# Low parts of every second expert block made by an accumulating DMA instead of GpSimd or VectorE

## The chip, the cores and the metric

The kernel runs on one core of a Trainium2 chip. The metric is the device time of one execution in microseconds (us). Its engines are TensorE (PE in the rows; PEld is its weight load), VectorE (DVE), ScalarE (ACT), GpSimd (POOL) and SyncE (SP, which here only issues DMAs).

## The reference, cut to what matters

A two-layer network on 512 positions of width 1024, all in float32. Each layer is a mixer followed by a PEER sub-layer, a retrieval among 128 x 128 = 16384 one-neuron experts:

```python
def block(xb):                                   # 128 positions
    q = (xb @ wq).reshape(128, 8, 2, 128)
    s1 = einsum('phd,kd->phk', q[:, :, 0], k1)   # scores of 128 keys, twice
    s2 = einsum('phd,kd->phk', q[:, :, 1], k2)
    ...                                          # top 16 of each, top 16 of their sums
    ue, ve = u_tab[eid], v_tab[eid]              # 8 heads x 16 experts per position
    act = gelu(einsum('pd,phkd->phk', xb, ue))
    return einsum('phk,phkd->pd', softmax(top_s) * act, ve)
```

## The kernel before, in words

For three of the four tiles of 128 positions (384 columns) the kernel does not gather: it multiplies by all experts and weighs by a mostly empty matrix. A block is one first key, 128 experts. `u_item(b)` multiplies the block's 128 x 1024 rows of `peer_u` by the activations and leaves the GELU in `act`; `v_item(b)` multiplies the weighted GELUs by `peer_v` and sums in `acc`. The fourth tile's rows are gathered with indirect DMAs (`gather`, buffers `grow_`), issued by GpSimd and consumed by VectorE.

To keep float32 precision, every weight is split into a high part (the value rounded to `F32R`) and a low part (what is left), and a product is three matmuls (`mm3`, L125 to L128): high by high, high by low, low by high. `weights` loads a block into `raw` (SyncE's queue), ScalarE writes `hi` by a copy (L112), and VectorE or GpSimd writes `lo = raw - hi` (L115). The third matmul of a block's first k (L128, `u<-hh,lo`) is the first to read `lo`. `raw` has two buffers, `hi` and `lo` three each. The argument `sub` says who subtracts:

```python
raw = st.tile([P, D], F32, name="raw", bufs=2)
nc.sync.dma_start(out=raw, in_=src)
hi = st.tile([P, D], F32R, name="hi", bufs=3)
lo = st.tile([P, D], F32R, name="lo", bufs=3)
split(hi, lo, raw, A, sub)
```

The PEER part of a layer runs in this order:

- The query loop: 16 blocks of `wq`; blocks 1 and 10 (`j % QM == 1`) get their low part from GpSimd.
- The first expert loop: `u_item` for blocks 0 to 31 (`FIRST` = 32). GpSimd subtracts for the odd blocks, VectorE for the even ones. After block 8i VectorE ranks the last scores (`best`), after block 8i + 1 it runs `pick` for one tile of positions: the top 16 of the sums, the softmax and the indices, with one exponential on ScalarE (L576) and three transposes on TensorE (L620 to L622). `ahead(items, n)` writes the loads of block b + n ahead of block b's matmuls. In this loop the order on each engine is set by the framework's planner, which goes by priority (the order of the code) and by the times that it reckons.
- The hand-ordered steps (`manual_schedule`): `PLAN` lists blocks 32 to 63 of u with 2 gathers, 64 blocks of v with 100, blocks 64 to 127 of u with 58, and 64 blocks of v with the rest. `run` prepares the weights of step i + 2 (`LOOK`) in the middle of step i (`meanwhile`), together with `spread` (small matmuls that make the weight matrix, L683 and L684), `weigh` (L698, L700) and `onehots` (L668 to L675). VectorE subtracts in all these steps.

In both, buffers are handed out when the program is planned: a new tile takes the buffer that the plan frees first, and its first writer waits for the last reader of that buffer.

Of the kernel before, what the change touches and what calls it, by code (L numbers as in the profile page):

```python
# [10 lines left out]
F32 = mybir.dt.float32  # L11
# [5 lines left out]
AF = mybir.ActivationFunctionType  # L17
OP = mybir.AluOpType
# [19 lines left out]
CH = NK // 2  # L38
# [14 lines left out]
UM = 2  # L53
# [3 lines left out]
FIRST = 2 * UNIT  # L57
# [9 lines left out]
def trunk(ctx: ExitStack, tc: tile.TileContext, x, rows1, rows2, ada, w_qk, w_row, w_o, wq, kt, wst,  # L67
          vnorm, fnorm, ut, u_rows, v_rows, out):
    nc = tc.nc
    V, A, G, T = nc.vector, nc.scalar, nc.gpsimd, nc.tensor  # L70
# [39 lines left out]
    def split(dst_hi, dst_lo, src, eng=A, sub=V):  # L110
        if eng is A:
            A.activation(dst_hi, src, AF.Copy)  # L112
        else:
            V.tensor_copy(dst_hi, src)  # L114
        sub.tensor_tensor(dst_lo, src, dst_hi.bitcast(F32), OP.subtract)  # L115

    def weights(src, sub=V):
        raw = st.tile([P, D], F32, name="raw", bufs=2)
        nc.sync.dma_start(out=raw, in_=src)
        hi = st.tile([P, D], F32R, name="hi", bufs=3)  # L120
        lo = st.tile([P, D], F32R, name="lo", bufs=3)
        split(hi, lo, raw, A, sub)
        return hi, lo

    def mm3(o, lh, ll, rh, rl, first, last):  # L125
        T.matmul(o, lh, rh, start=first, stop=False)  # L126
        T.matmul(o, lh, rl, start=False, stop=False)  # L127
        T.matmul(o, ll, rh, start=False, stop=last)  # L128

    def ahead(items, n=1):  # L130
        ready = []
        for i in range(len(items) + n):
            if i < len(items):
                ready.append(items[i][0]())
            if i >= n:
                items[i - n][1](ready.pop(0))
# [82 lines left out]
    def mixer(l):  # L219
        with tc.tile_pool(name="mx", bufs=1) as mx:  # L220
# [29 lines left out]
            with tc.tile_pool(name="pps", bufs=8, space=PSUM) as ps, tc.tile_pool(name="nm", bufs=1) as nm:  # L250
# [23 lines left out]
                def qk_item(j):  # L274
                    def use(w):
                        wh, wl = w
                        pq = ps.tile([P, S], F32, name="b")
                        for k in range(KD):
                            sl = slice(k * P, (k + 1) * P)
                            mm3(pq, wh[:, sl], wl[:, sl], hh[:, k], hl[:, k], k == 0, k == KD - 1)  # L280
                        A.activation(qk[:, j], pq, AF.Copy, scale=0.125 if j < 4 else 1.0)
                        fill(2)
                    return lambda: weights(w_qk[l, j]), use

                def row_items(src, evict):
                    pr = {}

                    def item(kk):
                        def use(w):
                            wh, wl = [a.rearrange("p (a b) -> p a b", a=2) for a in w]  # L290
                            for t in range(NTT):
                                if kk == 0:
                                    pr[t] = ps.tile([P, 512], F32, name="b")
                                ts = slice(t * P, (t + 1) * P)
                                for i in range(2):
                                    k = 2 * kk + i
                                    mm3(pr[t], hh[:, k, ts], hl[:, k, ts], wh[:, i], wl[:, i],
                                        k == 0, k == KD - 1)
                                if kk == 3:
                                    evict(t, pr[t])  # L300
                            fill(2)
                        return lambda: weights(src[kk]), use
                    return [item(kk) for kk in range(4)]
# [103 lines left out]
            with tc.tile_pool(name="ops", bufs=8, space=PSUM) as ps, tc.tile_pool(name="rg", bufs=1) as rg:  # L407
                po = {}

                def out_item(half, kk):  # L410
                    def use(w):
                        wh, wl = [a.rearrange("p (a b) -> p a b", a=2) for a in w]
                        for t in ORDER:
                            if kk == 0:
                                po[t] = ps.tile([P, 512], F32, name="b")
                            ts = slice(t * P, (t + 1) * P)
                            for i in range(2):
                                k = 2 * kk + i
                                mm3(po[t], hh[:, k, ts], hl[:, k, ts], wh[:, i], wl[:, i], k == 0, k == KD - 1)
                            if kk == 3:  # L420
                                residual(row[0], po[t], t, half, mx.tile([P, 512], F32, name="tk", bufs=2))
                                if half == 1:
                                    stats(t, y[:, t])
                                    nc.sync.dma_start(out=xd[t], in_=held["xs"][:, t])
                        if half == 0 and kk == 0:
                            ynorm(ps, 1)
                            row[0] = gate_rows(rg.tile([P, D], F32, name="grow"), ps, "b", l, 0)
                        fill(3)
                    return lambda: weights(w_o[l, half, kk]), use

                row = [None]
                ahead([out_item(half, kk) for half in range(2) for kk in range(4)])
                fill(96)

    def peer(l):
        with tc.tile_pool(name="pe", bufs=1) as pe, \
# [19 lines left out]
            def spot(b):  # L456
                a, i = slot(b)
                return act[a][:, i]

            def u_item(b):  # L460
                def use(w, meanwhile=None):
                    uh, ul = w
                    turn[0] ^= 1
                    pu = ups.tile([P, 512], F32, name=f"u{turn[0]}")
                    for k in range(KD):
                        if k == MID and meanwhile is not None:
                            meanwhile()
                        sl = slice(k * P, (k + 1) * P)
                        mm3(pu[:, :ND], uh[:, sl], ul[:, sl], hh[:, k, :ND], hl[:, k, :ND], k == 0, k == KD - 1)
                    w, n = spot(b), gone[b]  # L470
                    if n:
                        g = pe.tile([P, ND], F32, name="gu", bufs=1)
                        A.activation(g[:, :n], pu[:, :n], AF.Gelu_apprx_tanh)  # L473
                        late.append(lambda: V.tensor_mul(w[:, :n], w[:, :n], g[:, :n]))
                    if n < ND:
                        A.activation(w[:, n:], pu[:, n:ND], AF.Gelu_apprx_tanh)  # L476
                    known[b] = True
                return lambda: weights(ut[l, b], G if b < FIRST and b % UM == 1 else V), use

            with tc.tile_pool(name="tk", bufs=1) as tk, \  # L480
                    tc.tile_pool(name="tps", bufs=6, space=PSUM) as ps:
# [52 lines left out]
                def best(t, j0, s):  # L534
                    for jj in range(4):
                        j = j0 + jj
                        V.max(vals[t][:, j, 0:8], s[:, jj])
                        V.max_index(idx[t][:, j, 0:8], vals[t][:, j, 0:8], s[:, jj])
                        V.match_replace(s[:, jj], vals[t][:, j, 0:8], s[:, jj], NEG)
                        V.max(vals[t][:, j, 8:16], s[:, jj])  # L540
                        V.max_index(idx[t][:, j, 8:16], vals[t][:, j, 8:16], s[:, jj])
# [4 lines left out]
                with tc.tile_pool(name="pk", bufs=1) as pk:  # L546
# [82 lines left out]
                    def u_after(b):  # L629
                        prep, use = u_item(b)  # L630

                        def also(w):
                            use(w)
                            if b % 8 == 0:
                                best(*ranked.pop(0))
                            if b % 8 == 1:
                                pick(order[b // 8])
                        return prep, also

                    ahead([u_after(b) for b in range(FIRST)])  # L640

            with tc.tile_pool(name="gp", bufs=1) as gp, ExitStack() as psc:
                iot = gp.tile([P, P, SUB], F16, name="iot")
# [189 lines left out]
    for l in range(L):  # L833
        mixer(l)
        peer(l)
# [49 lines left out]
```

## Time and profile before

| | |
|---|---|
| median of 3 runs | 3236.4 us (3232.05 to 3236.57) |
| the profiled execution's own time | 3243.2 us |
| its span, first to last instruction | 3241.5 us |
| mean granted TensorE clock | 0.969 of full speed |
| busy: PE, DVE, ACT, POOL | 93%, 78%, 36%, 28% of the span |

All rows below are from the one profiled execution. A time of an engine's work is when the instruction ran; a DMA row's time to landing runs from its issue to the arrival of its last byte. Matmuls are pipelined, so the durations of successive ones overlap.

### The profile page before, as it was taken

The page shows a single profiled execution, that of the slowest core. Times are in us where ns is not written, and L with a number is a line of the kernel's source. Part 1 is how long each engine was busy: PE and PEld are TensorE (multiplying, and loading weights), DVE is VectorE, ACT ScalarE, POOL GpSimd, SP SyncE. Part 2 cuts the span into 40 slices and gives each one's busy share as a digit, 9 for nine tenths or more (in the row PEclk, how much of TensorE's full clock was granted, in tenths as well). Part 3 has the DMA queues.
Part 4 walks back from the last instruction along what each step waited for, and adds up shares of the span by engine and source line. Part 5 has one row for each costly group of instructions (what it writes and reads, how often), then busy time and mean ns, then how long its engine had stood idle before and what let it go on. Part 6 is the DMA issues. An engine that isn't in the chain of part 4 may idle for free. (4 is left out here: it accounts for less than half of the span.)

```text
span 3241.5 us, 46943 instructions
## 1 busy us (share of the span) xinstructions
PE 3022.1 (93%) x17516; PEld 2641.6 (81%) x17516; DVE 2536.8 (78%) x4973; ACT 1176.6 (36%) x2016; POOL 906.7 (28%) x602
## 2 busy tenths in 40 slices
PE   6998988999999999989989989889999999999897
PEld 5786887998777999867777878889977789997776
DVE  7677799698778889778744448979887788887787
ACT  3353333333333433323333533334333334333333
POOL 1001022103445223345410010220055432334452
PEclk8988999999999999999999899999999999999999
DMA  8746222337888666688732022233388876667885
GB/s 304 250 144 203 79 85 99 123 107 245 296 298 296 229 228 224 235 303 305 269 97 82 9 98 79 98 117 103 116 309 296 290 280 224 222 221 273 304 298 201
DMA packets 178840, 651.45 MB, mean 201 GB/s; under 512 B 19851, under 2 KB 20275, under 8 KB 178611
## 3 DMA queue, kind: packets, MB, share of 16 engines
q1 hardware_dynamic: 104018, 378.14, 34.2%
q0 software_dynamic: 73728, 268.47, 23.0%
q8 instruction: 137, 2.24, 0.3%
q10 hardware_dynamic: 864, 1.84, 0.2%
q14 instruction: 93, 0.75, 0.1%
HBM read 642.08 MB, written 6.29 MB: 200 GB/s over the span
## 5 line engine op out<-in xcount | busy, mean ns | idle before, releaser
L112 ACT ACTIVATE hi<-raw 128x1024 fp32r<-128x1024 f32 x600 | 635.9, 1060 | 1338.6 <-DMA raw<-in_v_rows 449.7
L115 DVE TENSOR_TENSOR lo<-raw,hi 128x1024 fp32r<-128x1024 f32 x564 | 699.0, 1240 | 230.8 <-ACT hi L112 229.6
L126 PE MATMUL u<-hh,hi 128*128 128x384 f32 x2048 | 706.4, 345 | 6.3 <-ACT act L476 6.3
L128 PE MATMUL u<-hh,lo 128*128 128x384 f32 x2048 | 692.8, 338 | 7.2 <-DVE lo L115 7.2
L127 PE MATMUL u<-hl,hi 128*128 128x384 f32 x2048 | 692.7, 338 | 0.0
L128 PE MATMUL acc<-hi,hl 128*128 128x512 f32 x1536 | 616.1, 401 | 63.1 <-DVE hl L115 61.4
L126 PE MATMUL acc<-hi,hh 128*128 128x512 f32 x1536 | 605.1, 394 | 9.7 <-ACT hh L112 9.7
L127 PE MATMUL acc<-lo,hh 128*128 128x512 f32 x1536 | 602.4, 392 | 0.0
L128 PEld LDWEIGHTS acc<-hi,hl 128*128 128x128 f32 x1536 | 290.4, 189 | 172.3 <-DVE hl L115 113.4
L128 PEld LDWEIGHTS u<-hh,lo 128*128 128x128 f32 x2048 | 389.9, 190 | 9.1 <-DVE lo L115 9.1
L126 PEld LDWEIGHTS u<-hh,hi 128*128 128x128 f32 x2048 | 390.3, 191 | 7.0 <-ACT act L476 6.9
L127 PEld LDWEIGHTS u<-hl,hi 128*128 128x128 f32 x2048 | 390.7, 191 | 0.1
L126 PEld LDWEIGHTS acc<-hi,hh 128*128 128x128 f32 x1536 | 290.8, 189 | 69.9 <-ACT hh L112 13.8
L127 PEld LDWEIGHTS acc<-lo,hh 128*128 128x128 f32 x1536 | 291.0, 189 | 62.0
L115 POOL TENSOR_TENSOR lo<-raw,hi 128x1024 fp32r<-128x1024 f32 x36 | 97.1, 2696 | 476.2 <-ACT hi L112 453.0
L126 PE MATMUL b<-hh,hi 128*128 128x512 f32 x384 | 150.7, 396 | 18.2 <-DVE hh L114 17.5
L127 PE MATMUL b<-hl,hi 128*128 128x512 f32 x384 | 150.3, 393 | 0.5 <-DVE hl L115 0.5
L128 PE MATMUL b<-hh,lo 128*128 128x512 f32 x384 | 150.1, 391 | 0.0
L190 DVE SCALAR_TENSOR_TENSOR aw<-aw,crow 128x1024 f32<-128x1024 f32 x96 | 119.1, 1244 | 37.8 <-DMA aw<-in_ada 37.5
L115 DVE TENSOR_TENSOR hl<-act,hh 128x384 fp32r<-128x384 f32 x256 | 140.9, 550 | 3.2 <-ACT hh L112 3.2
L473 ACT ACTIVATE gu<-u 128x384 f32<-128x384 f32 (+23 forms) x186 | 63.9, 343 | 208.9 <-PE u L128 208.3
L112 ACT ACTIVATE hh<-act 128x384 fp32r<-128x384 f32 x256 | 129.9, 508 | 4.8 <-PE acc L127 4.8
(1508 smaller groups left out, 4804.5 us busy)
## 6 DMA issues: line engine op xcount, KB each, us to landing
raw<-in_ut SPq DMA_DIRECT2D x256, 512.0 KB, 3.5
raw<-in_v_rows SPq DMA_DIRECT2D x256, 512.0 KB, 4.8
aw<-in_ada SPq DMA_DIRECT2D x96, 512.0 KB, 4.4
raw<-in_wq SPq DMA_DIRECT2D x32, 512.0 KB, 3.5
raw<-in_w_row SPq DMA_DIRECT2D x24, 512.0 KB, 4.4
raw<-in_w_qk SPq DMA_DIRECT2D x16, 512.0 KB, 3.4
raw<-in_w_o SPq DMA_DIRECT2D x16, 512.0 KB, 4.5
xd<-xs SPq DMA_DIRECT2D x8, 512.0 KB, 4.0
```

What stands on the lines that cost most here:

```text
L112: A.activation(dst_hi, src, AF.Copy)
L115: sub.tensor_tensor(dst_lo, src, dst_hi.bitcast(F32), OP.subtract)
L126: T.matmul(o, lh, rh, start=first, stop=False)
L127: T.matmul(o, lh, rl, start=False, stop=False)
L128: T.matmul(o, ll, rh, start=False, stop=last)
L190: V.scalar_tensor_tensor(aw, aw, 1.0, crow[0], op0=OP.mult, op1=OP.mult, accum_out=modc[:, l, j:j + 1])
L473: A.activation(g[:, :n], pu[:, :n], AF.Gelu_apprx_tanh)
```

## The change

Where `weights` is told that GpSimd makes the low part (`sub is G`), GpSimd no longer subtracts. ScalarE writes the high part, then a second time with the sign turned into `lo`, and a DMA issued by GpSimd adds `raw` onto `lo` in SBUF. This holds for the two query blocks of each layer too. The odd blocks that go this way now reach up to block 63 (`CH` = 64) instead of 31, so 32 instead of 16 per layer; blocks 33 to 63 were VectorE's before. And the first expert loop writes its loads two blocks ahead instead of one.

```diff
@@ weights @@
         lo = st.tile([P, D], F32R, name="lo", bufs=3)
-        split(hi, lo, raw, A, sub)
+        if sub is G:
+            A.activation(hi, raw, AF.Copy)
+            A.activation(lo, hi.bitcast(F32), AF.Copy, scale=-1.0)
+            G.dma_start(out=lo, in_=raw, accum_op=OP.add)
+        else:
+            split(hi, lo, raw, A, sub)
         return hi, lo
@@ u_item @@
-                return lambda: weights(ut[l, b], G if b < FIRST and b % UM == 1 else V), use
+                return lambda: weights(ut[l, b], G if b < CH and b % UM == 1 else V), use
@@ peer @@
-                    ahead([u_after(b) for b in range(FIRST)])
+                    ahead([u_after(b) for b in range(FIRST)], 2)
```

## Rows read from the trace of the kernel before

**Rows 1.** The page, busy time by engine: us, share of the span, instructions

```profile
span 3241.5 us, 46943 instructions
...
PE 3022.1 (93%) x17516; PEld 2641.6 (81%) x17516; DVE 2536.8 (78%) x4973; ACT 1176.6 (36%) x2016; POOL 906.7 (28%) x602
```

**Rows 2.** Busy time by stage, blocks 0-31 and 32-63, layers 0 and 1

```profile
core 0: us, PE busy (x) PEld busy (x) DVE busy (x) ACT busy (x) POOL busy (x), PEclk, DMA share, GB/s
428.00:604.00 176.00, 151.41 (x828) 148.40 (x826) 154.04 (x583) 60.28 (x80) 46.20 (x20) 0.91 0.31 105
604.00:762.00 158.00, 158.00 (x1513) 153.04 (x1510) 141.37 (x220) 63.60 (x174) 5.02 (x3) 1.00 0.35 114
2019.00:2195.00 176.00, 151.05 (x831) 148.21 (x830) 154.75 (x587) 60.68 (x81) 45.97 (x20) 0.93 0.31 105
2195.00:2353.00 158.00, 158.00 (x1511) 153.01 (x1510) 141.38 (x220) 63.50 (x174) 5.12 (x3) 1.00 0.34 114
```

**Rows 3.** What TensorE waited for, 428 to 604: us, times, longest

```profile
PE b L620 <- DVE f L607: 11.6, 3, 5.5
PE b L621 <- DVE f L612: 6.4, 2, 5.8
PE u L128 <- DVE lo L115: 3.5, 2, 2.9
PE u L126 <- ACT act L476: 3.1, 1, 3.1
```

**Rows 4.** Groups by line, three of 428 to 604, then one of 604 to 762

```profile
L115 POOL TENSOR_TENSOR lo<-raw,hi 128x1024 fp32r<-128x1024 f32 x15 | 41.4, 2762 | 105.3 <-ACT hi L112 99.2 <-DVE pos L572 6.2
L112 ACT ACTIVATE hi<-raw 128x1024 fp32r<-128x1024 f32 x32 | 33.9, 1060 | 102.0 <-PE u L127 54.6 <-DMA raw<-in_ut 34.5 <-POOL lo L115 7.1
...
L115 DVE TENSOR_TENSOR lo<-raw,hi 128x1024 fp32r<-128x1024 f32 x17 | 25.2, 1484 | 19.5 <-ACT hi L112 19.5
...
L115 DVE TENSOR_TENSOR lo<-raw,hi 128x1024 fp32r<-128x1024 f32 x32 | 39.0, 1220 | 8.0 <-ACT hi L112 7.9
```

**Rows 5.** Instructions of GpSimd and VectorE in order of time: start, us

```profile
441.89 4.52 POOL L115 TENSOR_TENSOR lo<-raw,hi 128x1024 fp32r<-128x1024 f32 x1 [5.75 <-ACT hi L112]
444.26 3.23 DVE L602 TENSOR_TENSOR pr<-th,dif 128x2048 f16<-128x2048 f16 x1
...
481.86 1.21 DVE L602 TENSOR_TENSOR pr<-th,dif 128x2048 f16<-128x2048 f16 x1
...
560.10 3.10 POOL L115 TENSOR_TENSOR lo<-raw,hi 128x1024 fp32r<-128x1024 f32 x1 [5.21 <-ACT hi L112]
561.02 3.25 DVE L115 TENSOR_TENSOR lo<-raw,hi 128x1024 fp32r<-128x1024 f32 x1
```

**Rows 6.** What SyncE's queue waited for, 428 to 604: us, times, longest

```profile
SPq L119 <- POOL lo L115: 50.4, 10, 9.0
SPq L119 <- DVE lo L115: 45.3, 9, 10.2
```

**Rows 7.** ScalarE, GpSimd, VectorE and SyncE in order of time, 585 to 593

```profile
585.83 1.06 ACT L112 ACTIVATE hi<-raw 128x1024 fp32r<-128x1024 f32 x1 [2.67 <-PE u L127]
...
586.97 2.38 POOL L115 TENSOR_TENSOR lo<-raw,hi 128x1024 fp32r<-128x1024 f32 x1 [5.86 <-ACT hi L112]
...
589.38 0.33 SPq L119 DMA_DIRECT2D raw<-in_ut  x1
...
590.04 1.06 ACT L112 ACTIVATE hi<-raw 128x1024 fp32r<-128x1024 f32 x1 [2.77 <-PE u L127]
...
591.13 1.23 DVE L115 TENSOR_TENSOR lo<-raw,hi 128x1024 fp32r<-128x1024 f32 x1 [7.09 <-ACT hi L112]
...
592.39 0.33 SPq L119 DMA_DIRECT2D raw<-in_ut  x1
```

**Rows 8.** DMA issues: count, KB each, us from issue to landing

```profile
raw<-in_ut SPq DMA_DIRECT2D x256, 512.0 KB, 3.5
...
grow__10650<-in_v_rows,ids POOLq DMA_INDIRECT x1, 4.2
...
grow__7119<-in_u_rows,ids POOLq DMA_INDIRECT x1, 5.9
...
grow__7549<-in_u_rows,ids POOLq DMA_INDIRECT x1, 9.7
```

**Rows 9.** Busy time by stretch, as rows 2: three gathers, gathers at full load

```profile
579.00:580.00 1.00, 1.00 (x8) 1.00 (x7) 0.00 (x0) 0.00 (x0) 1.00 (x1) 1.00 0.94 352
...
750.00:1050.00 300.00, 286.90 (x1247) 231.32 (x1247) 236.71 (x347) 100.15 (x136) 147.41 (x102) 0.99 0.84 294
```

**Rows 10.** GpSimd's issue of a gather, twice, and VectorE beside the second

```profile
574.93 0.94 POOL L728 DMA_INDIRECT grow__7048<-in_u_rows,ids  x1 [0.30 <-issue]
...
678.07 2.00 POOL L728 DMA_INDIRECT grow__7119<-in_u_rows,ids  x1 [88.71 <-DVE grow__5960 L731]
...
678.02 1.23 DVE L115 TENSOR_TENSOR lo<-raw,hi 128x1024 fp32r<-128x1024 f32 x1 [0.22 <-ACT hi L112]
```

**Rows 11.** Busy time by stretch, as rows 2: the query loop

```profile
320.00:430.00 110.00, 107.42 (x539) 91.26 (x538) 82.08 (x454) 37.97 (x57) 5.69 (x4) 0.99 0.23 77
```

## The prediction

> **What bounds the kernel now.** I read the totals first [rows 1]: TensorE (PE) is busy for 93% of the span, VectorE (DVE) for 78%, ScalarE for 36%, GpSimd for 28%. That is an average over unlike stages, so I cut out the stages that the diff touches. They are the same in both layers: the top-k loop over blocks 0 to 31 (428 to 604 us, and 2019 to 2195), and the hand-ordered steps over blocks 32 to 63 (604 to 762, and 2195 to 2353) [rows 2]. The reader is to see two different limits. In blocks 32 to 63 PE is busy for 158.00 of 158 us at full clock: nothing waits there, and nothing that frees another engine can shorten it. In blocks 0 to 31 PE is idle for 24.6 us, at a mean clock of 0.91. The waits say why: 11.6 + 6.4 us for DVE's top-k results (`pick`'s transposes), 3.5 us for a low part, 3.1 us for a GELU behind a table load, together all of the 24.6 [rows 3]. So `pick` on DVE sets the pace of the first loop. Per pair of blocks the first loop takes 176 / 16 = 11.0 us, the second 158 / 16 = 9.9 us.
>
> **What GpSimd costs DVE today.** In the first loop 15 low parts run on GpSimd at 2.76 us and 17 on DVE at 1.48 us; the same DVE instruction takes 1.22 us in blocks 32 to 63, where GpSimd subtracts nothing [rows 4]. The instructions in order of time show what happens: while GpSimd subtracts from 441.89, a DVE product lasts 3.23 us, and 1.21 us where GpSimd is still; at 560.10 a DVE subtraction lasts 3.25 us [rows 5]. Nine such meetings in one layer's first loop (these are the first and the last) add about 2 us each, I count 17 us. Taking GpSimd's arithmetic away gives DVE these 17 us per layer back. It cannot save more than that by itself, so the first loop's floor is 176 - 17 = 159 us.
>
> **What the change adds.** Every odd block of 0 to 63 (32 per layer) and two query blocks per layer go another way: load raw, high part on ScalarE (1.06 us [rows 4]), a second ScalarE pass of the same shape that writes the negated high part (1.06 us by the same row), then a DMA issued by GpSimd that reads raw, reads and writes lo. ScalarE's extra 68 x 1.06 = 72 us lie on an engine that is busy for a third of the span: nothing. DVE loses 16 subtractions of 1.22 us per layer in blocks 32 to 63: nothing, since PE is full there.
>
> What counts is how long one raw buffer is held. There are two, and consecutive blocks take them in turn: in the first loop SyncE waited 10 times for a GpSimd and 9 times for a DVE subtraction [rows 6]. The trace shows the hand-over: GpSimd ends at 586.97 + 2.38 = 589.35 and the next odd load is issued at 589.38; DVE ends at 592.36 and the next even load goes at 592.39 [rows 7]. After the change the odd buffer is free only when the accumulating DMA has landed, since the DMA reads raw. So an odd load, the two ScalarE passes and the accumulation form a ring that runs once per pair of blocks, and no lookahead shortens it: load 3.5 us to landing [rows 8], 1.06 + 1.06, about 0.1 for hand-overs (0.03 each above), together 5.7 us, plus the accumulation's time from issue to landing, L. Today the same ring takes 3.5 + 1.06 + 2.4 to 2.8, about 7.2 us. Where nothing stalls, high parts start 4.1 to 4.2 us apart [rows 7], so a pair takes 8.3 us, and ScalarE's wait for PE at 585.83 and 590.04 shows that PE is what it waits for. The ring is hidden in blocks 32 to 63 only while 5.7 + L is under 9.9, so L under 4.2.
>
> **L.** The trace has no accumulating DMA and no transfer within SBUF. The nearest rows are GpSimd's 512 KB gathers, issued by the same queue: 4.2 us the fastest, 5.9 the median of the 170 listed, 9.7 the slowest [rows 8]. GpSimd itself is busy with one issue for 0.94 us where DVE rests, and for 2.00 us beside a DVE subtraction [rows 10]; DVE hardly rests in the first loop. The lower bound is 4.2, the upper 9.7. The accumulation also reads its destination, another 524 KB; while the gathers of 573 to 577 landed, the DMA engines moved 352 GB/s [rows 9], so 1.5 us more if the reads don't overlap, 7.4 in all. I take 6.6, halfway between 5.9 and 7.4.
>
> The Trainium skill would make L smaller: DMA: Bandwidth & Descriptors, section "Anatomy of one DMA", fits a DMA issued by GpSimd with 2.0 us plus the bytes over 436e3 per us, an estimate of 3.2 us for 512 KB. By that the ring would take 8.9 us and hide, and the kernel would end at the time of the first rival below, which is this rule worked out in rows; the gathers here land in 5.9 us at the median, so the trace does not bear it out.
>
> **The sum.** The ring takes 5.7 + 6.6 = 12.3 us per pair. Blocks 0 to 31: 16 x 12.3 = 197 us instead of 176, +21; DVE's 17 us are gained and hidden behind the ring. Blocks 32 to 63: 197 instead of 158, +39. The query blocks take 110 us for 16 [rows 11], 13.8 a pair, more than 12.3: 0. The larger lookahead (`ahead(..., 2)`): 0, because buffers, not the order of the code, already set when a high part starts; at best it moves a high part ahead of the exponential in ScalarE's queue and saves the 3.1 us above, which the ring hides. Waits: GpSimd's accumulation waits for ScalarE's second pass; behind it in GpSimd's queue stand only the next accumulations and three gathers whose consumers come many blocks later, 0. Behind SyncE's waiting odd load stands the even load; it then goes 0.33 us later and has a whole block left, 0. Where PE idles its clock may fall, as the mean of 0.91 in the first loop shows, but a pair of 8.3 to 9.9 us has over 2 us of room in the ring, 0. Together +60 per layer, +120 for two. The profiled execution took 3243.2 us (its span is 3241.5), so 3363; it lies 6.8 us above the median of the runs, 3236.4, so I predict **3356 us**, 3.7% slower.
>
> **Rivals.**
> *Hidden, faster.* L is at most 4.2, as for the fastest gather. The ring then takes 9.9 us or less, blocks 32 to 63 stay at 158, and DVE's 17 us per layer show: 2 x 17 = 34 less, 3202 us. For it: lo and raw both lie in SBUF, and nothing comes from HBM. Against it: one gather of 170 landed that fast, and none also read its destination. It decides from L under 4.7, where 32 x (5.7 + L) = 176 + 158.
> *Buffers change places, faster.* A buffer goes to the next load in the order in which buffers are planned to come free. If the even subtraction is planned to end before the odd accumulation, the next odd load takes the even buffer, each buffer serves odd and even by turns, and a pair needs (12.3 + 3.5 + 1.06 + 1.22) / 2 = 9.0 us, under 9.9: again 3202. For it: the odd hold outlasts the even one by 6.5 us. Against it: the even high part starts a block, 4.1 to 5 us, later, which leaves under 2.4 us between the two ends, and the turns are strict today [rows 6].
> *No change.* L near 4.7: the first loop gains what the second loses, 3236.
> *Slow accumulation.* L at the slowest gather's 9.7, say because reading and rewriting the destination serialise: the ring is 15.4, 246 us per loop, +70 + 88 per layer, 3236 + 316 = 3552. The 9.7 us gather lies in a stretch in which the DMA engines are busy for 84% [rows 9]; here they are at a third [rows 2], which speaks against it.
>
> **Chances and range.** The ring with L from 5.2 to 8.5: 0.66, its times 3236 + 2 x (32 x 10.9 - 334) = 3266 to 3476. Slow accumulation beyond that: 0.10. Hidden: 0.10. Buffers change places: 0.09. No change: 0.05. So slower by over 0.2% 0.76, within 0.2% 0.05, faster by over 0.2% 0.19; 0.2% (6.5 us) is about what the runs, 4.5 us apart, can tell. The range 3200 to 3475 takes in the two faster cases and leaves out the slow one and a little beside. The likeliest case alone: 3266 to 3476.
>
> **What would show it.** Right: in blocks 32 to 63 PE idle for some 35 to 45 us per layer, waiting at every odd block's third matmul (L128) for the DMA into lo; SyncE waiting for that same DMA before each odd load; odd loads 12 us apart; DVE's products at 1.2 us and its subtractions at 1.22 everywhere. Wrong: PE at 158 of 158 again, or L under 4.7. If stalls appear and the odd loads do not wait for the accumulation, the ring is the wrong mechanism even where the time fits.

## The result and the profile after

The changed kernel takes 3265.5 us (median of 4 runs, 3262.0 to 3268.3), the kernel before 3236.5 (4 runs, 3232.1 to 3240.1): a ratio of 1.0077, 95% interval 1.0058 to 1.0095. It is slower, by 29 us. The forecast was slower by 120.

First the page of the changed kernel: span, busy time by engine, a group of TensorE's matmuls, and the new DMA (count, KB, us from issue to landing); then the landing times of that DMA in the hand-ordered steps of layer 0.

```profile
span 3266.5 us, 47116 instructions
...
PE 3034.5 (93%) x17516; PEld 2641.5 (81%) x17516; DVE 2468.8 (76%) x4941; ACT 1250.0 (38%) x2084; POOL 868.7 (27%) x634
...
L133 PE MATMUL u<-hh,lo 128*128 128x384 f32 x2048 | 697.1, 341 | 51.4 <-DMA lo<-raw 51.1
...
lo<-raw POOLq DMA_DIRECT2D x68, 512.0 KB, 4.6
```

```profile
DMA to landing us min/median/max: 4.5/4.6/6.0
```

Beside [rows 1], DVE has 68 us less to do and ScalarE 73 more. The third matmul of a block (L133 now) waits 51.1 us in all for a DMA that did not exist. That DMA lands after 4.6 us, not after the 6.6 of the forecast.

Busy time by stage, columns as in [rows 2]: the first loop and the steps of layer 0, then of layer 1. Below it, TensorE's waits from 431 to 598 us and from 598 to 765, as in [rows 3].

```profile
431.00:599.00 168.00, 150.35 (x820) 144.53 (x819) 137.34 (x578) 77.19 (x95) 15.63 (x18) 0.96 0.56 150
599.00:765.00 166.00, 156.77 (x1501) 148.75 (x1498) 120.30 (x195) 78.06 (x186) 18.14 (x19) 1.00 0.57 151
2036.00:2207.00 171.00, 152.31 (x822) 146.31 (x822) 137.02 (x576) 77.30 (x95) 15.61 (x18) 0.95 0.55 145
2207.00:2377.00 170.00, 159.34 (x1500) 150.91 (x1495) 122.91 (x199) 78.13 (x187) 18.25 (x20) 0.99 0.57 153
```

```profile
PE u L133 <- DMA lo<-raw: 15.1, 12, 2.5
PE b L625 <- DVE f L612: 1.9, 2, 1.2
...
PE u L133 <- DMA lo<-raw: 9.5, 10, 2.4
```

The two stages went opposite ways. The steps over blocks 32 to 63, where TensorE had no idle time [rows 2], now hold waits for `lo`. The first loop became shorter: its waits for DVE's top-k results [rows 3] shrank from 18.0 to 1.9 us, but 15.1 us of waits for `lo` took their place. Two of DVE's groups in the first loop say why the first kind went: they are not stretched any more (3.23 and 3.25 us in [rows 5], and 1.48 at the mean of the subtractions in [rows 4]).

```profile
L115 DVE TENSOR_TENSOR lo<-raw,hi 128x1024 fp32r<-128x1024 f32 x16 | 19.5, 1221 | 23.1 <-ACT hi L112 23.1
L607 DVE TENSOR_TENSOR pr<-th,dif 128x2048 f16<-128x2048 f16 x4 | 4.9, 1218 | 0.0
```

For all kernels I took the stages' lengths from the instructions of the one profiled execution, in order of time: the first loop from its first `u` matmul to the first spread matmul, which stands in block 33, the steps from there to the first `acc` matmul. Layers 0 and 1, us; times are medians, ratios are to the kernel before on the same chip, with 95% intervals:

```
kernel                                    first loop     steps          time     ratio
before                                    175.4  174.9   154.5  154.5   3236.5
after                                     167.4  171.0   166.8  170.1   3265.5   1.0077 [1.0058, 1.0095]
e1  addend from HBM                       160.3  159.4   172.5  177.4   3251.0   1.0039 [1.0020, 1.0057]
e2  blocks 0-31 only                      169.1  177.5   154.5  154.5   3241.4   1.0005 [0.9981, 1.0029]
e3  lookahead 1                           167.1  171.6   166.8  169.5   3260.3   1.0058 [1.0035, 1.0081]
e4  plain copy, nothing added             157.7  158.7   155.5  155.5   3207.9   one run
e5  prepared early                        167.5  166.2   174.4  178.4   3285.6   1.0135 [1.0107, 1.0163]
e6  prepared early, from HBM              160.4  159.8   162.9  162.6   3236.5   0.9974 [0.9955, 0.9993]
e7  from HBM, blocks 0-31 only            160.7  160.7   154.5  154.5   3212.4   0.9897 [0.9854, 0.9939]
e8  two halves                            168.9  168.0   172.7  171.6   3264.5   1.0068 [1.0044, 1.0093]
e9  odd ones early                        165.6  170.1   172.5  178.7   3271.7   1.0091 [1.0068, 1.0113]
e10 odd ones early, from HBM              156.9  159.5   166.5  163.9   3233.7   0.9981 [0.9963, 0.9999]
e11 from HBM, every block of 0-31         166.2  165.1   154.5  154.5   3208.6   0.9889 [0.9866, 0.9911]
e12 as e10, no gathers in the steps       160.3  159.6   160.1  160.9   3226.5   0.9957 [0.9930, 0.9985]
```

From before to after these stages give -8.0 - 3.9 + 12.3 + 15.6 = +16.0 us of the 25.0 by which the two spans differ. The other 9 lie in stretches that vary by as much between kernels with the same code there (over the twelve experiments 423.9 to 433.9 us before the first loop, and 1249 to 1269 between the two layers' stages), so I give them no cause. The first loop varies too: with the changed kernel's code it took 165.6 to 177.5 us (after, e2, e5, e9), so its -8.0 and -3.9 are one draw of a gain of a few us. With the addend from HBM for its odd blocks (e1, e6, e7, e10, e12) it took 156.9 to 160.7.

### The profile page after: what moved, and what is told of

Read it like the earlier page. It is cut to its first block, busy times and chain, and to the rows that moved or that the text cites. A ratio compares the mean times of both kernels' runs of the same rounds, so it can differ in the third digit from the quotient of the medians.

```text
span 3266.5 us, 47116 instructions
## 1 busy us (share of the span) xinstructions
PE 3034.5 (93%) x17516; PEld 2641.5 (81%) x17516; DVE 2468.8 (76%) x4941; ACT 1250.0 (38%) x2084; POOL 868.7 (27%) x634
## 5 line engine op out<-in xcount | busy, mean ns | idle before, releaser
L112 ACT ACTIVATE hi<-raw 128x1024 fp32r<-128x1024 f32 x532 | 563.5, 1059 | 1128.6 <-DMA raw<-in_v_rows 418.7
L115 DVE TENSOR_TENSOR lo<-raw,hi 128x1024 fp32r<-128x1024 f32 x532 | 649.3, 1221 | 232.5 <-ACT hi L112 231.3
L133 PE MATMUL u<-hh,lo 128*128 128x384 f32 x2048 | 697.1, 341 | 51.4 <-DMA lo<-raw 51.1
L133 PE MATMUL acc<-hi,hl 128*128 128x512 f32 x1536 | 614.0, 400 | 69.9 <-DVE hl L115 68.6
L133 PEld LDWEIGHTS u<-hh,lo 128*128 128x128 f32 x2048 | 389.3, 190 | 67.1 <-DMA lo<-raw 66.8
L133 PEld LDWEIGHTS acc<-hi,hl 128*128 128x128 f32 x1536 | 289.6, 189 | 176.5 <-DVE hl L115 118.6
L125 POOL DMA_DIRECT2D lo<-raw x68 | 59.7, 878 | 856.2 <-ACT lo L124 382.1
L133 PE MATMUL b<-hh,lo 128*128 128x512 f32 x384 | 149.8, 391 | 0.0
```

The costliest lines, as they stand in the source:

```text
L125: G.dma_start(out=lo, in_=raw, accum_op=OP.add)
```

## The experiments

**Which way is the long one in the steps?** The instructions of the changed kernel in order of time show one turn (start, us, engine):

```profile
646.01 0.87 POOL L125 DMA_DIRECT2D lo<-raw  x1 [10.67 <-ACT gu L478]
652.08 0.45 PE L133 MATMUL u<-hh,lo 128*128 128x384 f32 x1 [1.48 <-DMA lo<-raw]
652.09 0.80 SPq L119 DMA_DIRECT2D raw<-in_ut  x2
654.22 0.37 ACT L705 ACTIVATE act<-g 128x80 f32<-128x80 f32 x2 [3.32 <-DVE act L703]
655.81 1.06 ACT L123 ACTIVATE hi<-raw 128x1024 fp32r<-128x1024 f32 x1 [1.22 <-DMA raw<-in_ut]
656.90 1.06 ACT L124 ACTIVATE lo<-hi 128x1024 fp32r<-128x1024 f32 x1
658.26 0.87 POOL L125 DMA_DIRECT2D lo<-raw  x1 [11.37 <-ACT gu L478]
```

When the DMA lands, two things start in the same moment: the waiting matmul, and the next loads into `raw`. From the landing one way leads over the load (3.72 us to the high part), two passes of 1.06, 0.30 to the issue at 658.26, and 4.6 to the next landing: 10.8 us for two blocks, the ring of the forecast. The other leads over the matmul, the spread and the weighing (L703, L705) to the same high part: without the 1.22 us in which ScalarE waited for `raw` it takes 4.96 us to the issue, 9.6 with the transfer.

Both have to hide behind two blocks of matrix work. The steps begin within block 33, so their 154.5 us are less than 16 pairs (the 9.7 us a pair of an expectation below is too low). From the third matmul of block 33 to that of block 63 there are 15 pairs; first the kernel before, then the changed one:

```profile
602.79 0.33 PE L128 MATMUL u<-hh,lo 128*128 128x384 f32 x1
754.15 0.33 PE L128 MATMUL u<-hh,lo 128*128 128x384 f32 x1
```

```profile
597.90 0.44 PE L133 MATMUL u<-hh,lo 128*128 128x384 f32 x1 [0.23 <-DMA lo<-raw]
761.57 0.44 PE L133 MATMUL u<-hh,lo 128*128 128x384 f32 x1 [2.40 <-DMA lo<-raw]
```

That is 151.4 us and 163.7, 10.1 us a pair and 10.9; the 12.3 us between them are the whole loss of these steps. So one way, at 10.8, is over the limit of 10.1, and the other, at 9.6, half a microsecond under it; the experiments have to tell which one sets the time.

**e1.** The ring is opened: the addend comes from HBM, so `raw` is free after the high part.

```diff
-            G.dma_start(out=lo, in_=raw, accum_op=OP.add)
+            G.dma_start(out=lo, in_=src, accum_op=OP.add)
```

> The accumulating DMA adds the block from HBM (a second read of the same 512 KB) instead of from the raw buffer, so that raw is free after the high-part pass; nothing else changes. Ring theory (the odd raw buffer, held until the accumulation lands, sets the pace of blocks 32 to 63): their time falls from 172 and 175 us per layer to 158 to 161, TensorE's waits for the DMA into lo nearly vanish there, and the kernel takes 3225 to 3240 us. Lead theory (the low part is late because its own chain, high part, negation, accumulation, is longer than the two blocks by which the high part runs ahead): the chain is as long as before or longer, since HBM is read, so the stalls stay and the kernel takes 3262 to 3275 us.

The first loop fell to 160 us, as the ring has it. The steps became longer still, which neither theory expected. In order of time, one turn of them:

```profile
643.13 0.44 PE L133 MATMUL u<-hh,lo 128*128 128x384 f32 x1 [0.61 <-DMA lo<-in_ut]
...
644.70 0.52 DVE L703 SCALAR_TENSOR_TENSOR act<-g,act 128x344 f32<-128x344 f32 x1 [0.81 <-PE g L689]
645.25 0.37 ACT L705 ACTIVATE act<-g 128x80 f32<-128x80 f32 x2 [2.44 <-DVE act L703]
645.51 1.06 ACT L123 ACTIVATE hi<-raw 128x1024 fp32r<-128x1024 f32 x1
646.61 1.06 ACT L124 ACTIVATE lo<-hi 128x1024 fp32r<-128x1024 f32 x1
...
647.96 0.88 POOL L125 DMA_DIRECT2D lo<-in_ut  x1 [10.11 <-PE u L133]
...
654.63 0.45 PE L133 MATMUL u<-hh,lo 128*128 128x384 f32 x1 [1.20 <-DMA lo<-in_ut]
```

No high part waits for `raw`; the way over the weighing takes 4.83 us from landing to issue, and the transfer from HBM 6.7: 11.5 us a turn here. Opening the ring made the transfer longer and so the other way binding. That alone does not say which way binds in the changed kernel.

**e2.** Only blocks 0 to 31 go the new way.

```diff
-                return lambda: weights(ut[l, b], G if b < CH and b % UM == 1 else V), use
+                return lambda: weights(ut[l, b], G if b < FIRST and b % UM == 1 else V), use
```

> Only blocks below 32 take the accumulating DMA; VectorE subtracts again in blocks 33 to 63. Both theories: blocks 32 to 63 return to 158 to 160 us per layer, which takes some 29 us off, and the first loop keeps its gain of 8 and 4 us. If the late gathers at the start of the v steps (5 to 6 us in layer 0) come from GpSimd's queue standing behind accumulations, they go too: 3225 to 3232 us in all; if not, 3232 to 3237.

The steps return to 154.5 us and the time to that of before: the whole loss comes from blocks 33 to 63. The first loop does not keep its gain in both layers (169.1 and 177.5 us), and the time shows none that can be told.

**e3.** The lookahead of the first loop is put back.

```diff
-                    ahead([u_after(b) for b in range(FIRST)], 2)
+                    ahead([u_after(b) for b in range(FIRST)])
```

> The lookahead of the first expert loop goes back to one block. As predicted (buffers, not the order of the code, set when a high part starts): no change, 3260 to 3270 us. Rival: with one block ahead the odd block's two ScalarE passes stand behind pick's exponential and the planner puts accumulations later, the first loop loses its gain and takes 170 us or more per layer: 3275 to 3290 us.

The four stages differ from the changed kernel's by 0.6 us at most. The lookahead does nothing that can be told.

**e4.** The DMA copies `raw` onto `lo` and adds nothing; the low part is then the whole value.

```diff
-            G.dma_start(out=lo, in_=raw, accum_op=OP.add)
+            G.dma_start(out=lo.bitcast(F32), in_=raw)
```

> GpSimd's DMA writes raw over the negated high part instead of adding it, so the low part is the whole value and the output is not the reference's; the number of instructions is the same. It measures what reading the destination costs. If the accumulation pays for its third stream of 512 KB (1 to 1.5 us by the busiest rate seen), the DMA lands in 3.1 to 3.6 us instead of 4.6 and blocks 32 to 63 take 158 to 162 us. If reading the destination overlaps, 4.4 to 4.7 us, and these blocks take 168 to 175 us as in the changed kernel.

A DMA that only copies, in order of time; behind it the load that waits for its landing:

```profile
641.85 0.54 POOL L125 DMA_DIRECT2D lo<-raw  x1 [9.56 <-PE u L133]
...
644.75 0.33 SPq L119 DMA_DIRECT2D raw<-in_ut  x1
```

The copy frees `raw` 2.9 us after its issue (the median of 13 turns from 601 us on; 2.89 to 4.28, where a load may have waited for something else too), where the adding DMA takes 4.6. Ring and other way are then 1.7 us shorter and both hidden: steps 155.5, first loop 158. So the 1.7 us that the addition adds to this transfer decide 48 us over the four stages (675.3 and 627.4). The Trainium skill has a rule near this: Collectives: The Full Stack, section "The bandwidth ceiling: the fold count and why AG ≠ RS ≠ AR", says of a ReduceScatter, a collective whose DMAs add, that it is slower because the add reads two sources. With the fit cited in the prediction and the bytes counted twice this gives an estimate of 4.4 us, and 3.2 for the copy; the runs show 4.6 and 2.9, which is near both. That the second read is the cause of the 1.7 us here is not shown.

**e5.** The weights of block i + 2 are prepared ahead of the weighing, which shortens the other way and leaves the ring.

```diff
+                        if len(steps[i][0]) == 2:
+                            prepare(i + LOOK)
                         for part in fresh:
                             weigh(*part)
...
-                        prepare(i + LOOK)
+                        if len(steps[i][0]) > 2:
+                            prepare(i + LOOK)
```

> The changed kernel, but in the hand-ordered steps of the first half the weights of block i + 2 are prepared ahead of the weighing of block i's spread chunk, not behind it. Two theories of the 166.8 and 170.1 us of these steps (154.5 before the change). Ring theory: the two raw buffers bind (load 3.5 to 3.8, hi pass 1.06, negation 1.06, hand-over 0.3, transfer 4.6, together 10.5 to 10.8 us per pair of blocks against 9.7 of matrix work), so the order on ScalarE is no matter and the steps stay at 164 to 172 us, time 3258 to 3270. Lead theory: what binds is the way from the start of an odd block over spread, weighing, hi pass, negation and transfer to the next odd block, which the earlier preparation shortens by 2 us or more: steps 154 to 160 us, time about 25 us under the changed kernel, 3232 to 3246. If both ways bind at about 10.6 us, the steps stay above 162.

The steps did not become shorter, but 8 us longer, above what was expected of the ring too. This speaks against the other way as the cause. But TensorE also waited once for a one-hot table. I put that down to VectorE's subtractions for the even blocks, which stood ahead of the tables now; e9 moves the odd blocks alone.

**e9.**

```diff
+                    def early(i):
+                        return i < CH - FIRST and i % UM == 1
...
-                        if len(steps[i][0]) == 2:
+                        if early(i):
                             prepare(i + LOOK)
...
-                        if len(steps[i][0]) > 2:
+                        if not early(i):
                             prepare(i + LOOK)
```

> As the first earlier preparation with raw as the source, but only the odd blocks (whose weights VectorE doesn't touch) are prepared ahead of the weighing; the even blocks keep their place, so that no one-hot table comes late. Ring theory (raw's two buffers bind at 10.4 to 10.7 us a pair): steps 166 to 171 us, ScalarE's hi passes wait 25 us or more for raw, matrix work no longer for lo; time 3258 to 3270. Lead theory alone: steps 154 to 158 us, 3235 to 3245.

What ScalarE waited for in the steps, first in the changed kernel, then in e9:

```profile
ACT hi L123 <- DMA raw<-in_ut: 12.5, 13, 3.4
```

```profile
ACT hi L123 <- DMA raw<-in_ut: 28.2, 12, 5.1
```

The high part now stands ready earlier and only waits longer for `raw`: 28.2 us instead of 12.5, and with it all that is queued behind it on ScalarE. TensorE's waits for `lo` fall from 9.5 to 3.8 us, but the wait for a one-hot table is still there, 5.7 us, so the even blocks were not its cause (e10 shows it). With that wait the steps lie above the ring's 166 to 171 us, and it covers waits for `lo` that would have come behind it. So I count only up to it: over the first 16 blocks from the first spread matmul, 81.5 us in the kernel before, the changed kernel loses 5.8 and 7.1 us in the two layers and e9 4.0 and 6.5. With the other way shortened most of the loss is still there: the ring sets the steps of the changed kernel, and the other way adds at most the rest.

**e6 and e10.** The edits of e5 and of e9, each together with that of e1: neither way is left.

> The same earlier preparation, and the adding DMA takes its addend from the weights in HBM, so that raw is free after the hi pass. Neither way is left. Lead theory and the two-ways theory: steps 154 to 158 us (172.5 and 177.4 with the HBM source alone), loop 1 as with the HBM source alone, 158 to 162 us (175 before), time 3205 to 3220, faster than both kernels. Ring theory of the first kind (raw binds, nothing else) can't explain the 172.5 and 177.4 us of the HBM source alone and would expect no change from them: 3250.

> The same for the odd blocks alone, with the HBM source. Both ways are open: steps 154.5 to 157 us (162.9 and 162.6 when the even blocks were moved too, 172.5 and 177.4 with the HBM source and the order unchanged), loop 1 160 us, time 3205 to 3220. If what kept the steps above 154.5 us was the transfer of 5.9 us and not the late one-hot tables, the steps stay at 160 to 163 us and the time at 3225 to 3240.

The steps fall to 163 and 164 to 166 us, against 172 to 177 in e1, but not to the 154 to 158 expected. So in e1 the order on ScalarE did bind. What is left above 154.5 shows in e10 in order of time:

```profile
657.31 0.88 POOL L125 DMA_DIRECT2D lo<-in_ut  x1 [9.64 <-ACT act L705]
658.50 1.09 POOL L733 DMA_INDIRECT grow__5993<-in_u_rows,ids  x1 [0.31 <-issue]
...
666.49 1.22 DVE L736 SCALAR_TENSOR_TENSOR grow__5993<-grow__5993,hrow 128x1024 f32<-128x1024 f32 x1 [9.84 <-DMA grow__5993<-in_u_rows,ids]
...
671.44 0.21 PE L688 MATMUL g<-wide 128*128 128x64 f16 x1 [4.78 <-DVE wide L680]
```

One row gather stands behind an adding DMA in GpSimd's queue. Its consumer on VectorE waits 9.84 us, and the one-hot table behind that keeps TensorE waiting. (In e9 VectorE waited 10.71 us for the same gather.)

**e12.** e10 with the two gathers of these steps moved to the next ones.

```diff
-PLAN = [("u", range(FIRST, CH), 1, 2),
-        ("v", [*range(NS1, CH), *range(NS1)], 0, 100),
+PLAN = [("u", range(FIRST, CH), 1, 0),
+        ("v", [*range(NS1, CH), *range(NS1)], 0, 102),
```

> As the odd blocks prepared early with the HBM source (steps 166.5 and 163.9 us), but the two row gathers of these steps moved to the following second-half steps. In that kernel VectorE once waited 9.8 us for a gathered row, whose gather was issued 1.2 us behind an adding DMA, and matrix work waited some 8 us for one-hot tables behind it. If that one wait is all that was left: steps 154.5 to 158 us, time 3207 to 3222. If the rest is the transfer of 6 to 7 us from HBM: steps 161 to 166 us, time 3228 to 3236.

Steps of 160.1 and 160.9 us: without that wait TensorE no longer waits for a one-hot table, 6.4 of the 12.0 us above 154.5 are gone in layer 0 and 3.0 of 9.4 in layer 1, and 6 us stay, between the two cases expected. In layer 0 most of them lie at the last odd block. TensorE's instruction and the busy time of two stretches there:

```profile
748.78 0.44 PE L133 MATMUL u<-hh,lo 128*128 128x384 f32 x1 [1.83 <-DMA lo<-in_ut]
```

```profile
746.00:748.70 2.70, 0.95 (x6) 0.63 (x4) 1.15 (x2) 1.84 (x3) 0.00 (x0) 1.00 1.00 281
...
750.00:754.00 4.00, 4.00 (x16) 4.00 (x15) 0.00 (x0) 0.00 (x0) 0.00 (x0) 0.57 0.90 367
```

TensorE waits 1.83 us while the DMA engines are busy for 100%, and about 1 us after the wait its granted clock is down to 0.57 of 2.4 GHz, near its lower level of 1.2: ten matmuls from 750 on start 0.32 us apart instead of 0.17, 1.5 us. For layer 1 I did not follow it.

**e8.** The adding DMA in two halves.

```diff
-            G.dma_start(out=lo, in_=raw, accum_op=OP.add)
+            for s in (slice(0, D // 2), slice(D // 2, D)):
+                G.dma_start(out=lo[:, s], in_=raw[:, s], accum_op=OP.add)
```

> The changed kernel with the adding DMA cut in two halves of 512 columns, 256 KB each. If a transfer's time is mostly its bytes and matrix work can start on the first half, the first half lands 2 us earlier, PE's waits for lo in the steps go and the lead loop opens, while raw is held as long as before: lead theory 3238 to 3250, ring theory no change, 3260 to 3270. If an adding DMA has a high fixed part (issue of 0.87 us each), the second half lands later than now and the kernel is slower, 3270 to 3290.

No change in the time, as expected of the ring. A row of its DMA issues in the steps, columns as in [rows 8]:

```profile
lo<-raw POOLq DMA_DIRECT2D x30, 256.0 KB, 4.1
```

Half the bytes take 4.1 us at the median (the second half's wait behind the first included) instead of 4.6: nothing is won by the cut.

**e7.** The addend from HBM, for blocks 0 to 31 alone; VectorE subtracts in the steps, as before.

```diff
-            G.dma_start(out=lo, in_=raw, accum_op=OP.add)
+            G.dma_start(out=lo, in_=src, accum_op=OP.add)
...
-                return lambda: weights(ut[l, b], G if b < CH and b % UM == 1 else V), use
+                return lambda: weights(ut[l, b], G if b < FIRST and b % UM == 1 else V), use
```

> The adding DMA with the HBM source only for the blocks of loop 1; blocks 33 to 63 as in the kernel before, with VectorE's subtraction. If the gain of loop 1 and the loss of the hand-ordered steps are independent: loop 1 158 to 162 us, steps 154.5 us, time 3205 to 3215. If the gain of loop 1 is given back later (VectorE's backlog, a busier DMA queue), 3230 to 3245.

Busy time by stage of layer 0, columns as in [rows 2], and TensorE's waits in the first of the two:

```profile
427.00:588.00 161.00, 146.21 (x823) 142.87 (x822) 137.46 (x577) 74.51 (x94) 17.94 (x20) 0.97 0.63 162
588.00:742.00 154.00, 154.00 (x1499) 149.75 (x1495) 138.03 (x214) 61.71 (x171) 3.50 (x2) 1.00 0.34 110
```

```profile
PE b L625 <- DVE f L612: 7.1, 2, 3.8
PE u L133 <- DMA lo<-in_ut: 4.9, 5, 2.0
PE b L626 <- DVE f L617: 2.9, 2, 2.4
```

Both gains are there and nothing is given back: the first loop 14 to 15 us shorter in each layer, the steps as before, 3212.4 us, 1.0% faster than the kernel before. VectorE's busy time in the first loop is 137.5 us instead of 154.0 [rows 2], and top-k is again what TensorE waits for most, as in [rows 3], but for 10.0 us instead of 18.0.

**e11.** As e7, for every block of 0 to 31.

```diff
-                return lambda: weights(ut[l, b], G if b < FIRST and b % UM == 1 else V), use
+                return lambda: weights(ut[l, b], G if b < FIRST else V), use
```

> The adding DMA with the HBM source for every block of loop 1, not for every second, and VectorE's subtraction in the steps. If loop 1 at 160 us is still set by VectorE: it falls toward the matrix work, 150 to 156 us, time 3195 to 3207. If the transfers of 5.9 us on one queue and two more passes of ScalarE bind (one block takes 5 us), loop 1 rises to 175 us or more: 3240 or above. If matrix work sets it already: within 2 us of the kernel with every second block, 3208 to 3216.

Landing times of the DMA in its first loop, and a row of TensorE's waits there:

```profile
DMA to landing us min/median/max: 5.5/7.1/12.2
```

```profile
PE u L133 <- DMA lo<-in_ut: 14.9, 10, 5.5
```

The first loop is 5 us longer than in e7: the top-k waits are nearly gone (3.5 us), but twice as many transfers take 7.1 us instead of 6.0 (both medians of the first loop) and up to 12.2, and TensorE waits for them. By its length none of the three cases expected came out (its time lies in the range of the third); the waits suggest a loop with two limits close to each other, which no run here separates. In time the two kernels can't be told apart (0.9889 and 0.9897, intervals overlapping).

## Why the sign was right and the size wrong

- **The step that failed is the term L.** I took 6.6 us for the adding DMA, between the median gather and that gather with a second read behind it. It measured 4.6. The rows I bounded it by are gathers from HBM; within SBUF a copy takes 2.9 us and the addition adds 1.7. The Trainium skill's estimate of 3.2 us, which I set aside, is near the copy; for an adding DMA it is too small, so neither number was right. By the prediction's own formula a ring of 5.7 + 4.6 = 10.3 us gives 16 x 10.3 = 165 us for each of the two stages, 330 a layer instead of 334: 3228 us, a little faster. So with this term alone put right the forecast would have had the wrong sign, and that it had the right one is in part luck.
- **The ring is the mechanism in the steps.** SyncE waits for this DMA before the odd loads, as the prediction asked for (all waits of its queue for it, 598 to 765: total, times, longest):

```profile
SPq L119 <- DMA lo<-raw: 137.8, 16, 11.4
```

  From block 37 on every odd load of these steps goes out 0.05 us after such a landing. High parts of odd blocks start 11.0 us apart there (600.27 to 754.29, 14 gaps), not 12.3. The 5.7 us that I put beside L measured 3.72 + 2 x 1.06 + 0.30, 6.1 us with 0.03 between the passes; the load took 0.2 longer than the 3.5 and the hand-over to GpSimd 0.30, not 0.03. e9 shows that the ring sets most of the time: shorten the other way and, up to the one-hot wait, little is won.
- **The room was read from a wrong cut.** The stretch from 604 to 762 us begins in block 33 and ends in the v steps. From block 33 to block 63 there are 15 pairs, not 16, at 10.1 us and not 9.9: 15 x (10.9 - 10.1) is the 12.3 us measured, where 16 x 10.9 - 158 gives 16. This is 4 us of the +39; the rest of what it has too much is L.
- **In the first loop the strict turns did not hold.** I forecast +21 and measured -8.0 and -3.9. The changed kernel, in order of time (an adding DMA had been issued at 451.34):

```profile
452.02 1.23 DVE L115 TENSOR_TENSOR lo<-raw,hi 128x1024 fp32r<-128x1024 f32 x1 [0.45 <-ACT hi L112]
453.27 0.33 SPq L119 DMA_DIRECT2D raw<-in_ut  x1
456.17 0.33 SPq L119 DMA_DIRECT2D raw<-in_ut  x1
457.68 1.06 ACT L123 ACTIVATE hi<-raw 128x1024 fp32r<-128x1024 f32 x1 [3.79 <-DMA raw<-in_ut]
```

  The load at 453.27, for an odd block, goes when VectorE's subtraction ends, while the adding DMA is still under way; the even load at 456.17 goes at its landing. Of the odd loads of blocks 3 to 31 in layer 0, 10 of 15 went like this and 5 at a landing: buffers do change places there, as the second rival has it (0.09, and meant for both stages). That loosens the ring: odd high parts start 10.3 us apart (436.41 to 590.67, 15 gaps), with the same transfer as in the steps. What is left of it cost TensorE the 15.1 us of waits for `lo`.
- **VectorE's 17 us** were right in size: 154.0 to 137.5 us of busy time in e7, 14 to 15 us of time. They were not hidden: they showed in part here, and e7, without the ring, has nearly all of them.
- **Costs put at nothing.** The lookahead: right (e3). The gathers behind the adding DMAs: right in this order, wrong in that of e9 and e10, 9.84 us for a single one. The query blocks can't be told from the spread of that stretch. ScalarE's extra 73 us: nothing as a load on the engine, as said; the second pass counts as 1.06 us of both ways.
- **Where the measured time lies.** L at 4.6 is on the faster side of the break-even of 4.7, and yet the four stages lost 16 us. The "no change" case at 0.05 lay nearest in L. That 3265.5 lies at the lower edge (3266) of the likeliest case is luck: this edge has a ring of 10.9 us in both stages, but only the steps have it, the first loop gained, and 9 us have no cause here.
- **Not foreseen:** a second way round, over spread and weighing, which the prediction did not list. At 9.6 us it lies half a microsecond under two blocks in the changed kernel and becomes the limit when the transfer grows to 6.7 (e1).

## What to carry to other kernels

When work moves from an engine into a DMA, add up every loop that the DMA closes, from its landing back to its issue, and compare each with the matrix work that covers it; opening one loop by a longer transfer may only hand the time to the next. Apply such a move where the relieved engine sets the pace (here blocks 0 to 31, 1.0% faster) and leave out stages in which the matrix engine is full. And price the new transfer by its own kind, where it reads from and how often, not by the nearest row in the same queue.

## What the runs showed of the hardware

- A 512 KB DMA issued by GpSimd took 2.9 us as a copy within SBUF, 4.6 as an addition within SBUF, and 5.6 to 7.3 (medians of a stage, e6, e7 and e10 to e12) as an addition from HBM with loads beside it. Its issue occupied GpSimd for 0.54 us as a copy and 0.87 as an addition.
- VectorE's subtractions and products with two inputs, stretched by about 2 us when they met a GpSimd subtraction, kept 1.2 us where they overlapped GpSimd's issue of an adding DMA (three subtractions and three products of the changed kernel).
